# Attention tiles in whole 128-row products, with one pass of scores that is turned, in a fused two-layer mixer and expert kernel

## The chip, the core and the metric

The kernel runs on one core of a Trainium2 chip. A core has TensorE (matrix products, out of SBUF into PSUM), VectorE, ScalarE and GpSimd for elementwise work, and DMA queues, most of them issued by SyncE. The metric is device time in microseconds of one execution of the whole program.

## The reference, cut to what matters

The program computes a block with three mixers side by side (an RWKV-7 recurrence, a sparse attention with three branches called NSA here, and a memory attention), an output projection, a second mixer, and 64 routed experts. Sequence 1024, width 1024; the query is handled in tiles of 128 rows, 8 in all. The change lies in the two attentions. With four heads of width 64:

```python
# compressed branch: 63 compressed keys
s_c = einsum('bqhd,bcd->bhqc', qn, k_cmp) * scale
p_c = masked_softmax(s_c, cmp_end <= tq)
o_c = einsum('bhqc,bcd->bqhd', p_c, v_cmp)
# selected branch: top 16 of 16 blocks of 64 keys, so all earlier keys
p_s = masked_softmax(einsum('bqhd,bqkd->bhqk', qr, kg) * scale, kpos <= tq)
o_s = einsum('bhqk,bqkd->bqhd', p_s, vg)
# local branch: a window of 512 keys
p_w = masked_softmax(einsum('bqhd,bkd->bhqk', qr, kwb) * scale, m_w)
o_w = einsum('bhqk,bkd->bqhd', p_w, vwb)
o = g0 * o_c + g1 * o_s + g2 * o_w          # then a norm per head and a gate
# memory attention: 256 keys, four heads of their own
prob = softmax(einsum('bthd,bmhd->bhtm', q, mem_k) * scale)
o = einsum('bhtm,bmhd->bthd', prob, mem_v)
```

## The kernel before, in words

**Streams.** The sequence is worked in two halves of 512 rows (H = 0, 1). Each piece of work is a generator that yields an estimate of its cost; `weave` always advances the generator whose sum of costs, times its rate, is lowest. So the costs behind `yield` set the order in which instructions are written down; outside the blocks under `manual_schedule` the engines' queues alternate more finely than the yields. Three weaves concern attention: in the first, `first_stage(0)` runs alone (projections of the recurrence, `derive`); in the second, `att_proj(0)`, `mem_kv`, `first_stage(1)` and `att_proj(1)` run beside `recur(0)` and `attend(0)`; in the third, `third_stage(0)` (output projection and second mixer of the first half) runs beside `recur(1)` and `attend(1)`, until these two end. `attend(H)` runs `mem_tile(i)` and `nsa_tile(i)` for the four query tiles i of its half. Then follow the rest of both halves, the router, and the experts, whose weights (64 x 3 x 2 MB) are loaded by `load_piece` (L1676). The first three of these loads wait for the router's index table of the first half (`idx0`); the experts' rows are gathered once the routing of both halves is known.

**Number forms.** A matrix product on data marked F32R is one pass; on F32 it is recorded as two instructions. To keep accuracy, operands are split in a high part rounded to F32R and the rest: `qh`, `ql` for queries (L954, L956), `ph`, `pl` for probabilities (L1064 to L1067). Keys of the selected and local branch, `ksT` and `kwT`, hold the high part in rows 0 to 63 and the rest in rows 64 to 127, and the queries hold the head twice, so that one product of 128 rows sums both.

**mem_tile.** Queries `mq` come as two pairs of heads, a head in each half of the rows. Scores (L916) are F32 products of 64 rows and 256 columns, four a tile; then a maximum, an exponential with its sum (L921), eight transposes (L930) and the product with the memory values (L937).

**nsa_tile, compressed branch.** Scores `pc` (L965) are F32 products of 64 rows against `kcT`, four a tile in two groups; softmax on all heads; two transposes (L977); the product `poc` with `vcm` (L985) is again four products of 64 rows, copied by ScalarE (L986).

**nsa_tile, selected and local branch.** With nb key blocks of 128 (i + 1 selected, at most 5 local; over all tiles 36 and 30), keys are cut in one chunk, or in two when nb is over 4. First pass, per head and chunk (L1012 to L1020): scores `pmx`, query by key, from `qh` and `ql`, a mask product on the last block (and the first of a full window), the negated maximum on VectorE, and an exponential on ScalarE, back into PSUM, of which only the sum is kept. The maxima of the 16 rows (two branches, four heads, high and low parts) are then transposed (L1038) and spread in a table `nmb` (L1044). Second pass, per block (L1057 to L1067): scores `pS`, key by query for four heads (512 columns), from `qh`, `ql` and a product of `ones` with `nmb`, which subtracts the maxima, and on 20 blocks in all a mask (L1061); the exponential is taken twice, rounded (`ph`) and full (`pf`), and the difference is `pl`. Both are multiplied with `vsw` (L1050), which holds the values' high part in 64 columns and the rest in the other 64, and summed over the blocks in `po`. At the end of a branch the two halves of `po` are added (L1077, L1078), four 64-row transposes turn the result (L1082), and it is weighted and added to `o`.

**Buffers.** Scores and turned pieces use the PSUM tag "s" (two banks), sums the tag "o" (one). SBUF tag "acc" has three buffers, "ph" and "pl" two each.

## Time and profile before

| what | value |
|---|---|
| median of 3 runs | 2548.81 us (2540.53 to 2549.47) |
| profiled execution | 2546.94 us, its span 2544.8 us |
| TensorE busy over the span | 2423.5 us (95%), 13518 products |
| VectorE, ScalarE, GpSimd busy | 1550.0 (61%), 772.7 (30%), 348.5 us (14%) |
| mean granted clock of TensorE | 0.979 |
| DMA | 603.67 MB, mean 237 GB/s |

Times in the trace count from the start of the span. Attention runs from about 300 to 970 us; the seam between the second and the third weave lies at 630 to 655 us. A matmul's length includes the drain of the array, and matmuls overlap, so the sum of lengths is not the time that they take from each other; the distance between starts is.

### The profile page before, as it was taken

What the parts mean: (1) busy time and instruction counts of PE and PEld (TensorE: products, weight loads), DVE (VectorE), ACT (ScalarE), POOL (GpSimd) and SP (SyncE); (2) the same over time, 40 slices, a digit from 0 to 9 for tenths busy, and PEclk for the clock granted to TensorE, in tenths of its full rate; (3) what the DMA queues carried; (4) which work ended last, traced back from release to release, by engine and by line L of the source; (5) the groups of instructions that cost most, each with busy time, mean ns of one, the idle gap of its engine ahead of it and who ended that gap; (6) DMA issues with size and microseconds to landing.
All of it is one profiled execution on the core that took longest, in us unless ns stands there. A gap on an engine that the chain in (4) does not pass through costs nothing. (4 is left out here: it accounts for less than half of the span.)

```text
span 2544.8 us, 36038 instructions
## 1 busy us (share of the span) xinstructions
PE 2423.5 (95%) x13518; PEld 1545.9 (61%) x13518; DVE 1550.0 (61%) x3104; ACT 772.7 (30%) x1516; POOL 348.5 (14%) x464
## 2 busy tenths in 40 slices
PE   8989999999988999999999969999999999999997
PEld 6766777777756767887878834444444444444443
DVE  5537666665776776676665646555555555555555
ACT  4423544434436543334242321111111111111112
POOL 3000000000001011101120020111111111111112
PEclk9989999999888999999999979999999999999999
DMA  7666544443523222445345668999999999999992
GB/s 166 163 148 192 144 106 123 109 121 94 177 59 117 73 70 71 133 136 170 116 139 196 248 237 358 410 408 412 412 409 412 410 408 412 410 410 408 408 410 84
DMA packets 352078, 603.67 MB, mean 237 GB/s; under 512 B 124408, under 2 KB 298112, under 8 KB 327328
## 3 DMA queue, kind: packets, MB, share of 16 engines
q1 hardware_dynamic: 344496, 592.53, 64.9%
q0 software_dynamic: 5168, 8.69, 1.1%
q8 instruction: 108, 1.77, 0.3%
q14 instruction: 66, 0.54, 0.1%
q10 hardware_dynamic: 2240, 0.14, 0.1%
HBM read 562.54 MB, written 47.25 MB: 240 GB/s over the span
## 5 line engine op out<-in xcount | busy, mean ns | idle before, releaser
L1738 PE MATMUL pgu<-mw,xT 128*64 128x512 f32 x2048 | 460.9, 597 | 2.3 <-DVE up L1743 2.3
L277 PE MATMUL pcm<-hTh,whi 128*128 128x512 f32 (+1 forms) x912 | 370.1, 406 | 0.2 <-DVE hTl L265 0.2
L277 PE MATMUL pcm<-hTh,wlo 128*128 128x512 f32 (+1 forms) x912 | 362.9, 398 | 0.4 <-DVE wlo L238 0.4
L277 PE MATMUL pcm<-hTl,whi 128*128 128x512 f32 (+1 forms) x912 | 360.8, 396 | 0.0
L237 ACT ACTIVATE whi<-wraw 128x512 fp32r<-128x512 f32 (+1 forms) x300 | 187.2, 625 | 458.8 <-PE pcm L277 318.0
L238 DVE TENSOR_TENSOR wlo<-wraw,whi 128x512 fp32r<-128x512 f32 (+1 forms) x300 | 211.4, 708 | 181.0 <-ACT whi L237 159.2
L1738 PEld LDWEIGHTS pgu<-mw,xT 128*64 128x64 f32 x2048 | 142.7, 137 | 265.6 <-issue 254.7
L1796 DVE TENSOR_TENSOR mw<-psp,mw 128x1024 f32<-128x1024 f32 x248 | 292.5, 1220 | 8.8 <-PE psp L1788 5.1
L1788 PE MATMUL psp<-yo,wt 128*128 128x512 f32 x1024 | 274.9, 410 | 4.1 <-DVE mw L1796 3.2
L1788 PEld LDWEIGHTS psp<-yo,wt 128*128 128x128 f32 x1024 | 182.8, 188 | 139.0 <-issue 80.6
L1766 PE MATMUL pyd<-mw,hT 128*64 128x512 f32 x1008 | 229.9, 598 | 2.3 <-DVEq L1929 2.3
L1742 DVE SCALAR_TENSOR_TENSOR mth<-mth,pgu 64x512 f32<-64x512 f32 x64 | 43.4, 679 | 291.6 <-ACT mth L1741 291.6
L277 PEld LDWEIGHTS pcm<-hTh,whi 128*128 128x128 f32 (+1 forms) x912 | 170.6, 187 | 41.4 <-issue 6.2
L277 PEld LDWEIGHTS pcm<-hTl,whi 128*128 128x128 f32 (+1 forms) x912 | 170.8, 187 | 39.3 <-issue 6.2
L277 PEld LDWEIGHTS pcm<-hTh,wlo 128*128 128x128 f32 (+1 forms) x912 | 170.2, 187 | 40.1 <-issue 2.3
L1741 ACT ACTIVATE mth<-pgu,rq 64x512 f32<-64x512 f32 x64 | 43.8, 684 | 491.8 <-PE pgu L1738 491.8
L1773 ACT ACTIVATE yo<-pyd,gt 64x512 fp32r<-64x512 f32 x128 | 87.6, 684 | 305.6 <-PE pyd L1766 304.3
L1775 DVE SCALAR_TENSOR_TENSOR yo<-pyd,gt,yo 64x512 fp32r<-64x512 f32 x128 | 95.9, 749 | 126.5 <-ACT yo L1773 125.4
L1781 POOL TENSOR_SCALAR wt<-rcon,tfs 128x128 fp32r<-128x128 f32 x256 | 150.3, 608 | 149.1 <-PE psp L1788 125.4
L1766 PEld LDWEIGHTS pyd<-mw,hT 128*64 128x64 f32 x1008 | 66.9, 136 | 126.7 <-issue 123.2
L1800 POOL DMA_INDIRECT xg<-d_x,idxt x32 | 34.4, 1074 | 688.6 <-issue 630.4
L1170 PE MATMUL pout<-whi,yh 128*128 128x512 f32 x256 | 107.7, 421 | 3.0 <-DVE rr L1173 3.0
(492 smaller groups left out, 3464.3 us busy)
## 6 DMA issues: line engine op xcount, KB each, us to landing
mw<-in_w_gate_dram SPq DMA_DIRECT2D x64, 2048.0 KB, 13.7
mw<-in_w_up_dram SPq DMA_DIRECT2D x64, 2048.0 KB, 9.6
mw<-in_w_down_dram SPq DMA_DIRECT2D x63, 2048.0 KB, 14.4
wraw<-in_w_in_dram SPq DMA_DIRECT2D x216, 256.0 KB, 3.2
wraw<-in_w_out_dram SPq DMA_DIRECT2D x32, 256.0 KB, 2.8
yr<-d_y SPq DMA_DIRECT2D x32, 256.0 KB, 3.0
d_x<-rr SPq DMA_DIRECT2D x16, 512.0 KB, 2.8
wraw<-in_w_o_dram SPq DMA_DIRECT2D x32, 256.0 KB, 2.9
```

The costliest lines, as they stand in the source:

```text
L237: nc.scalar.activation(hi, raw, AF.Copy)
L238: nc.vector.tensor_sub(lo, raw, hi.bitcast(F32))
L277: nc.tensor.matmul(ps[0:n], w, h[:, k], start=(k == 0 and j == 0), stop=(k == KD - 1 and j == 2))
L1170: nc.tensor.matmul(ps, y[:, t], w, start=(k == 0 and j == 0), stop=(k == 1 and j == 2))
L1738: nc.tensor.matmul(ph_[lohi[s]], xT[:, k], pieces[s][:, k * 512:(k + 1) * 512], start=(k == 0), stop=(k == KD - 1))
L1741: nc.scalar.activation(th, ph_[0:64], AF.Tanh, scale=rq[:, 0, h:h + 1])
L1766: nc.tensor.matmul(py[s][lohi[s]], hT[:, k, lohi[h]], piece[:, k * 1024 + s * 512:k * 1024 + s * 512 + 512], start=(k == 0), stop=(k == 3))
L1773: nc.scalar.activation(y[:, 0, 512 * s:512 * s + 512], py[s][o], AF.Copy, scale=gt[o, h:h + 1])
L1775: nc.vector.scalar_tensor_tensor(y[:, 1, 512 * s:512 * s + 512], py[s][o], gt[o, h:h + 1], y[:, 0, 512 * s:512 * s + 512].bitcast(F32), op ...
L1781: nc.gpsimd.tensor_scalar(w[0:n, i], iota[0:n], sh[0:n, i:i + 1], None, op0=OP.is_equal)
L1788: nc.tensor.matmul(ps[:, cs], w[0:n], yo[0:n, x, cs], start=(start and x == 0), stop=(x == 1))
L1796: nc.vector.tensor_tensor(x2, ps, x2, op=OP.add)
```

## The change: what it does

- Memory branch: queries are stored per head, the head twice (as for the selected branch), and split in `qh`, `ql` by a new helper `queries`; memory keys hold the high part and the rest in 128 rows. Scores are F32R products of 128 rows.
- Compressed branch: `kcT` and `vcm` are filled as block diagonals of two heads, so that one product of 128 rows serves two heads.
- Selected and local branch: the second pass is gone. The exponentials of the first pass are kept in SBUF; for each pair of heads and pair of blocks they are transposed into PSUM (`pTs`), split in `ph` and `pl` there, and multiplied with `vsw` in products of 256 columns. Each chunk has its own sum `po`, which is copied whole, turned by four 128-row transposes, and its halves are added then. Two chunks are joined by weights at the end of the branch.
- Beside that: `pa` in `derive` uses 128 rows, the lower half of its weights cleared by GpSimd; the table of maxima, `ones` and the transposed masks go; the compressed keys share a buffer with `Pw`; a junk tile moves.

```diff
     def derive(H, p, lora, tw, rest):
...
+        nc.gpsimd.memset(up[0:64, 1], 0.0)
...
-        nc.tensor.matmul(pa_, up[64:128, 1], lora[64:128], start=True, stop=True)
+        nc.tensor.matmul(pa_, up[:, 1], lora, start=True, stop=True)
...
     def compress(H):
...
+        kcv = wk1.tile([P, 16 + H2], F32, tag="Pw", name="kcv")
...
-        nc.vector.tensor_copy(kcT[H][:, 0:n], pk[:, 0:n])
+        for r in range(2):
+            nc.vector.tensor_copy(kcT[H][lohi[r], 64 * r:64 * r + n], pk[lohi[r], 0:n])
...
     def att_proj(H):
...
-            nc.sync.dma_start(d_mq[ts, :, c].rearrange("n q t -> q n t"), by_tile(s))
+            for b in range(2):
+                for o in lohi:
+                    nc.sync.dma_start(d_mq[ts, o, 2 * c + b].rearrange("n q t -> q n t"), by_tile(s[lohi[b]]))
...
+    def queries(src):
+
+        qd = at.tile([P, 4 * P], F32, tag="acc", name="qd", bufs=4)
+        nc.sync.dma_start(qd, src.rearrange("q h t -> q (h t)"))
+        qh = at.tile([P, 4 * P], F32R, tag="qh", name="qh")
+        nc.scalar.activation(qh, qd, AF.Copy)
+        ql = at.tile([P, 4 * P], F32R, tag="ql", name="ql")
+        nc.vector.tensor_sub(ql, qd, qh.bitcast(F32))
+        return qh, ql
+
     def mem_tile(i):
...
-            for c in range(2):
-                nc.tensor.matmul(ps[:, c * 256:(c + 1) * 256], mq[lohi[e], c], memk[lohi[e], c], start=True, stop=True)
+            for x in range(2):
+                h = 2 * j + x
+                for q in (qh, ql):
+                    nc.tensor.matmul(ps[:, x * 256:(x + 1) * 256], q[:, h * P:(h + 1) * P], memk[:, h],
+                                     start=q is qh, stop=q is ql)
...
     def nsa_tile(i):
...
-        for e in range(2):
-            ps = S1("pc")
-            for c in range(2):
-                nc.tensor.matmul(ps[:, c * 64:(c + 1) * 64], qn[lohi[e], c], kcT[H][lohi[e]], start=True, stop=True)
...
+        ps = S1("pc")
+        for c in range(2):
+            nc.tensor.matmul(ps[:, c * P:(c + 1) * P], qn[:, c], kcT[H], start=True, stop=True)
...
+        poc = S1("poc")
+        for c in range(2):
+            nc.tensor.matmul(poc[:, c * P:(c + 1) * P], pcT[:, c], vcm[H], start=True, stop=True)
...
+            for n, (u, v) in enumerate(zip(cut, cut[1:])):
...
+                po = O1("poT")
+                ready = []
+
+                def with_v():
+                    j, bs, parts = ready.pop(0)
+                    for k, b in enumerate(bs):
+                        for p_ in parts:
+                            nc.tensor.matmul(po[:, 256 * j:256 * j + 256], vsw[:, s0 + u + b, br], p_[:, 256 * k:256 * k + 256],
+                                             start=(b == 0 and p_ is parts[0]), stop=(b == v - u - 1 and p_ is parts[1]))
+                    return 0.302 * len(bs)
+
+                for j in range(2):
+                    prs = []
+                    for h in (2 * j, 2 * j + 1):
...
+                        m = mx[:, br, n, h:h + 1]
+                        nc.vector.tensor_reduce(m, ps[:, 0:w], axis=AX.X, op=OP.max, negate=True)
+                        pr = at.tile([P, 4 * P], F32, tag="acc", name="pr", bufs=4)
+                        nc.scalar.activation(pr[:, 0:w], ps[:, 0:w], AF.Exp, bias=m, accum_out=sm[:, br, n, h:h + 1])
+                        prs.append(pr)
+                        yield 0.2 * (v - u) + 0.2
+                        if ready:
+                            yield with_v()
+                    for g in range(0, v - u, 2):
+                        bs = range(g, min(g + 2, v - u))
+                        pt = S1("pTs")
+                        for k, b in enumerate(bs):
+                            for x in range(2):
+                                nc.tensor.transpose(pt[:, (2 * k + x) * P:(2 * k + x + 1) * P], prs[x][:, b * P:(b + 1) * P],
+                                                    ident)
+                        c = 256 * len(bs)
+                        ph, pl = [at.tile([P, 4 * P], F32R, tag=t, name=t, bufs=2) for t in ("ph", "pl")]
+                        nc.scalar.activation(ph[:, 0:c], pt[:, 0:c], AF.Copy)
+                        nc.vector.tensor_sub(pl[:, 0:c], pt[:, 0:c], ph[:, 0:c].bitcast(F32))
+                        yield 0.3 * len(bs)
+                        if len(ready) > 0:
+                            yield with_v()
+                        ready.append((j, bs, (ph, pl)))
+                yield 0.5
+                while ready:
+                    yield with_v()
+                oS = at.tile([P, 4 * P], F32R, tag="pl", name="oS", bufs=2).bitcast(F32)
+                nc.scalar.activation(oS, po, AF.Copy)
+                yield 0.3
+                pt = S1("pob")
+                for h in range(4):
+                    nc.tensor.transpose(pt[:, h * P:(h + 1) * P], oS[:, h * P:(h + 1) * P], ident)
...
-        for br, kT in enumerate((ksT, kwT)):
-            s0 = b0 if br else 0
-            nc.vector.tensor_tensor(nmb[0:16], nms[:, None, :].to_broadcast([16, 4, P]),
-                                    nsel[:, br, :, None].to_broadcast([16, 4, P]), op=OP.mult)
-            po = O1("poT")
...
-                nc.tensor.matmul(ps, blk, qh, start=True, stop=False)
-                nc.tensor.matmul(ps, blk, ql, start=False, stop=False)
-                nc.tensor.matmul(ps, ones, nmb.rearrange("p h t -> p (h t)"), start=False, stop=mask is None)
...
-                nc.scalar.activation(ph, ps, AF.Exp)
...
-                nc.scalar.activation(pf, ps, AF.Exp)
-                nc.vector.tensor_sub(pl, pf, ph.bitcast(F32))
```

## Rows read from the trace of the kernel before

**Rows 1.** Stretches: window, length; busy PE, PEld, DVE, ACT, POOL; PEclk, DMA share, GB/s.

```profile
300.00:630.00 330.00, 326.10 (x2214) 245.58 (x2213) 208.25 (x473) 149.69 (x330) 25.41 (x20) 0.99 0.43 108
630.00:655.00 25.00, 16.22 (x89) 12.83 (x89) 10.59 (x24) 8.10 (x18) 2.01 (x2) 0.66 0.64 207
655.00:810.00 155.00, 139.55 (x895) 99.59 (x893) 118.22 (x299) 79.10 (x181) 8.07 (x10) 0.90 0.36 107
810.00:970.00 160.00, 156.87 (x1144) 111.30 (x1143) 116.80 (x264) 85.03 (x199) 17.70 (x14) 1.00 0.25 71
970.00:1490.00 520.00, 501.87 (x2787) 410.99 (x2786) 338.09 (x735) 175.41 (x336) 65.17 (x70) 0.99 0.48 155
1550.00:2545.00 995.00, 966.30 (x4332) 438.31 (x4330) 554.42 (x807) 153.66 (x232) 186.62 (x296) 1.00 0.94 386
```

**Rows 2.** Timeline, TensorE, 831 to 832.6 us: start, length, line, operation, shapes, count.

```profile
831.37 0.66 PE L965 MATMUL pc<-kcT,qn 64*128 64x64 f32 x4
831.95 0.50 PE L277 MATMUL pcm<-hTh,whi 128*128 128x512 f32 x1
832.29 0.39 PE L277 MATMUL pcm<-hTl,whi 128*128 128x512 f32 x1
832.52 0.40 PE L277 MATMUL pcm<-hTh,wlo 128*128 128x512 f32 x1
```

**Rows 3.** Timeline, TensorE, 662 to 664 us.

```profile
663.51 0.28 PE L1012 MATMUL pmx<-ksT,qh 128*128 128x256 f32 x1
663.63 0.28 PE L1013 MATMUL pmx<-ksT,ql 128*128 128x256 f32 x1
```

**Rows 4.** Timeline, TensorE, 442 to 448 us.

```profile
443.31 0.44 PE L900 MATMUL pfin<-cst,on 128*128 128x128 f32 x2
443.68 1.90 PE L916 MATMUL pM<-memk,mq 64*128 64x256 f32 x8
445.51 0.50 PE L277 MATMUL pcm<-hTh,wlo 128*128 128x512 f32 x1
445.85 0.40 PE L277 MATMUL pcm<-hTh,whi 128*128 128x512 f32 x1
...
446.78 0.60 PE L930 MATMUL pTm<-cst,prm 128*128 128x128 f32 x4
447.13 0.48 PE L277 MATMUL pcm<-hTl,whi 128*128 128x512 f32 x1
447.45 0.40 PE L277 MATMUL pcm<-hTh,wlo 128*128 128x512 f32 x1
```

**Rows 5.** Timeline, TensorE, 623 to 625 us.

```profile
623.92 0.39 PE L1061 MATMUL pS<-maskb,identb 128*128 128x512 bf16 x1
623.96 0.58 PE L1050 MATMUL poT<-ph,vsw 128*128 128x512 f32 x1
624.38 0.39 PE L1050 MATMUL poT<-pl,vsw 128*128 128x512 f32 x1
```

**Rows 6.** Groups, TensorE, 285 to 970 us: shapes, count, busy us, mean ns.

```profile
L1059 PE MATMUL pS<-nmb,ones 128*128 128x512 f32 x66 | 26.4, 414 | 0.0
...
L1061 PE MATMUL pS<-maskb,identb 128*128 128x512 bf16 x20 | 7.8, 390 | 0.0
```

**Rows 7.** Timeline, TensorE, 517.2 to 518.8 us.

```profile
517.60 0.46 PE L1082 MATMUL pob<-cst,oS 64*128 64x64 f32 x4
517.99 0.50 PE L1057 MATMUL pS<-qh,kwT 128*128 128x512 f32 x1
```

**Rows 8.** Groups, all engines, 285 to 970 us.

```profile
L1067 DVE TENSOR_TENSOR pl<-pf,ph 128x512 fp32r<-128x512 f32 x66 | 45.6, 690 | 38.8 <-ACT pf L1066 34.5 <-PE pS L1059 3.5 <-PE pS L1058 0.5
...
L1066 ACT ACTIVATE pf<-pS 128x512 f32<-128x512 f32 x66 | 39.5, 599 | 0.0
```

**Rows 9.** Stretches, columns as in rows 1.

```profile
462.70:466.20 3.50, 2.89 (x28) 1.93 (x26) 3.45 (x9) 0.60 (x1) 0.00 (x0) 1.00 0.49 121
466.20:469.60 3.40, 3.40 (x7) 2.06 (x7) 3.39 (x9) 1.00 (x2) 0.00 (x0) 0.50 0.79 204
```

More of the change, by code (lines that the diff above doesn't have):

```diff
@@ L164, in body @@
     maskb = const.tile([P, _GOFF[1] - _GOFF[0]], BF, name="maskb")
[L165 removed]
+    causb, edgeb, beforeb, onesb = [maskb[:, x * P:(x + 1) * P] for x in range(4)]
     mhalf = const.tile([P, 64], F32, name="mhalf")
@@ L485, in body @@
     gl = res.tile([P, NT, 12], F32, name="gl")
-    kcv = res.tile([P, 16 + H2], F32, name="kcv")
+    kcl = res.tile([P, 16], F32, name="kcl")
     cact = res.tile([P, 64], F32, name="cact")
-    kcT, vcm = [[res.tile([P, 64], F32, name=f"{n}{H}") for H in range(2)] for n in ("kcT", "vcm")]
+    kcT, vcm = [[res.tile([P, P], F32, name=f"{n}{H}") for H in range(2)] for n in ("kcT", "vcm")]
     hgain = vcol(4)
@@ L564, in att_proj @@
         if H == 0:
-            for x in range(0, 6, 3):
-                masks = put()[:, 0:3 * P]
-                nc.sync.dma_start(masks, a["cst"][:, _GOFF[0] + x * P:_GOFF[0] + (x + 3) * P])
-                nc.vector.tensor_copy(maskb[:, x * P:(x + 3) * P], masks)
+            masks = put()
+            nc.sync.dma_start(masks, a["cst"][:, _GOFF[0]:_GOFF[1]])
+            nc.vector.tensor_copy(maskb, masks)
         rope = wk1.tile([P, 2, H2], F32, tag="xr", name="rope", bufs=2)
@@ L1004, in nsa_tile @@
             cut = [0, nb] if nb <= 4 else [0, (nb + 1) // 2, nb]
-            for h in range(4):
-                q = slice(h * P, (h + 1) * P)
-                for n, (u, v) in enumerate(zip(cut, cut[1:])):
-                    ps = S1("pmx")
-                    w = (v - u) * P
-                    ends, starts = v == nb, br == 1 and i >= 4 and u == 0
-                    rhs = kT[:, (s0 + u) * P:(s0 + v) * P]
-                    nc.tensor.matmul(ps[:, 0:w], qh[:, q], rhs, start=True, stop=False)
-                    nc.tensor.matmul(ps[:, 0:w], ql[:, q], rhs, start=False, stop=not (ends or starts))
-                    if starts:
-                        nc.tensor.matmul(ps[:, 0:P], identb, edgeb, start=False, stop=not ends)
-                    if ends:
-                        nc.tensor.matmul(ps[:, w - P:w], identb, causb, start=False, stop=True)
-                    m = mx[:, br, h, n:n + 1]
-                    nc.vector.tensor_reduce(m, ps[:, 0:w], axis=AX.X, op=OP.max, negate=True)
-                    nc.scalar.activation(ps[:, 0:w], ps[:, 0:w], AF.Exp, bias=m, accum_out=sm[:, br, h, n:n + 1])
-                yield 0.25 * nb
@@ L1022, in nsa_tile @@
-            if len(cut) > 2:
+            outs = []
+            for n, (u, v) in enumerate(zip(cut, cut[1:])):
+                w = (v - u) * P
+                ends, starts = v == nb, br == 1 and i >= 4 and u == 0
+                rhs = kT[:, (s0 + u) * P:(s0 + v) * P]
+                po = O1("poT")
[7 more added lines that the diff above has]
+                    return 0.302 * len(bs)
+                for j in range(2):
+                    prs = []
+                    for h in (2 * j, 2 * j + 1):
+                        q = slice(h * P, (h + 1) * P)
+                        ps = S1("pS")
+                        nc.tensor.matmul(ps[:, 0:w], qh[:, q], rhs, start=True, stop=False)
+                        nc.tensor.matmul(ps[:, 0:w], ql[:, q], rhs, start=False, stop=not (ends or starts))
+                        if starts:
+                            nc.tensor.matmul(ps[:, 0:P], identb, edgeb, start=False, stop=not ends)
+                        if ends:
+                            nc.tensor.matmul(ps[:, w - P:w], identb, causb, start=False, stop=True)
+                        m = mx[:, br, n, h:h + 1]
[10 more added lines that the diff above has]
+                        for k, b in enumerate(bs):
+                            for x in range(2):
+                                nc.tensor.transpose(pt[:, (2 * k + x) * P:(2 * k + x + 1) * P], prs[x][:, b * P:(b + 1) * P],
[17 more added lines that the diff above has]
+                    nc.tensor.transpose(pt[:, h * P:(h + 1) * P], oS[:, h * P:(h + 1) * P], ident)
+                pt = pt.rearrange("p (h x d) -> p h x d", h=4, x=2)
+                t = at.tile([P, 4, 64], F32, tag=("sc", "sqh")[n], name="ob")
+                nc.scalar.activation(t, pt[:, :, 0], AF.Copy)
+                nc.vector.tensor_tensor(t, pt[:, :, 1], t, op=OP.add)
+                outs.append(t)
+                yield 0.2
@@ L1087, in nsa_tile @@
+                nc.vector.tensor_tensor(m, sm[:, br, 0], sm[:, br, 1], op=OP.add)
+                weight(br + 1, m)
+                for n, t in enumerate(outs):
+                    nc.vector.tensor_tensor(mb[:, n], mb[:, n], den[:, :, br + 1], op=OP.mult)
+                    nc.vector.tensor_tensor(t, t, mb[:, n, :, None].to_broadcast([P, 4, 64]), op=OP.mult)
+            for t in outs:
+                nc.vector.tensor_tensor(o, o, t, op=OP.add)
         yield from finish_heads(i, o, 0)
```

125 lines of the change are left out of this document (33 added, 92 removed).

## The prediction, made before the changed kernel was run

> **What bounds the kernel now.** Read the stretches first [rows 1]. The columns that matter are TensorE's busy time, its granted clock and the DMA share. From 300 to 630 us TensorE is busy 326 of 330 us at a clock of 0.99; the other engines reach at most two thirds (VectorE 208 us, ScalarE 150). So the first half of attention is a queue of matmuls: what leaves that queue leaves the time. The same holds from 810 to 970 (157 of 160) and, for the stage behind attention, from 970 to 1490 (502 of 520). Between 630 and 655 (clock 0.66) and between 655 and 810 (140 of 155 us, clock 0.90) TensorE is not full: there the seam between the streams and the waits of attention on VectorE and ScalarE count too. From 1550 on the DMA engines are busy 0.94: the expert weights set the pace. Their loads wait for the routing, so that part starts as much earlier as attention ends earlier, and all of a gain or loss in front arrives at the end. The last chain of waits lies behind all this and says nothing of attention.
>
> The profiled execution took 2546.9 us (span 2544.8); the median of the three runs is 1.9 us above it. I make the sum against 2546.9 and add 1.9 at the end.
>
> **Prices.** "Busy" of a matmul includes its drain, so I price by the distance from one start to the next. A product of 512 columns costs 0.23 us (832.29 to 832.52 in [rows 2]), one of 256 columns 0.12, even where the weights change from qh to ql [rows 3]. Four 128x128 transposes take 0.35 us, and the product behind them 0.32 instead of 0.23: 0.44 together, 0.11 each [rows 4]. No row shows a 64-row product cheaper than one of 128 rows and as many columns, and it costs at both ends of its group: two transposes that should take 0.22 take 0.37 in front of one, and the 512-column product behind one takes 0.34 [rows 2, 4]. I take 0.2 us for entering and leaving. A mask over 512 columns shares 0.46 us with the next product, so it costs 0.23 [rows 5].
>
> **The sum on TensorE**, before to after:
> 1. The second pass of scores (L1057 to L1061) goes. It ran on 66 key blocks, with the products qh, ql and the maxima, 3 x 512 columns, and on 20 of them a mask [rows 6]. 66 x 3 x 0.23 + 20 x 0.23 = 50.1 us less. The first pass (L1012 to L1017) stays; its exponentials, of the same widths, go to SBUF now and are used.
> 2. These lie query by key and must be turned: four transposes a block, 264 x 0.11 = 29.0 us more.
> 3. The products with V have the same columns in pieces of 256: 264 x 0.12 - 132 x 0.23 = 1.3 us more.
> 4. The output is turned in whole rows, and once for each chunk: 24 chunks (two a branch in tiles 4 to 7, one in tiles 0 to 3) x 4 x 0.11 = 10.6 us, for 16 groups at 0.39 [rows 7] + 0.2 = 9.4: 1.2 us more.
> 5. Compressed scores: two groups of four fp32 instructions, 0.58 [rows 2] + 0.2 each, become four of 128 columns. The fp32 instruction of 256 columns took 1.83 / 8 = 0.23 [rows 4], so 128 columns are 0.115: 0.46. 8 tiles x (1.56 - 0.46) = 8.8 us less. Their product with V is one group in the code, priced as one of the above: 8 x (0.78 - 0.46) = 2.6 less.
> 6. Memory scores: 1.83 + 0.2 us [rows 4] of fp32 in 64 rows become eight single-pass products of 256 columns, 0.96: 8 x 1.07 = 8.6 less.
> 7. The eight `pa` products get 128 rows: 8 x 0.2 = 1.6 less. The transposed maxima (8 transposes) are under 1 us and left out.
> Sum: -50.1 + 29.0 + 1.3 + 1.2 - 8.8 - 2.6 - 8.6 - 1.6 = **-40.2 us** of TensorE.
>
> **The other engines.** ScalarE drops two exponentials of 512 columns a block, 132 x 0.60 = 79 us [rows 8], and gets a copy for each turned pair of blocks: counted from the chunk sizes there are 54 groups of 512 columns and 24 of 256, at most 78 x 0.60 = 47. Output copies (24 of full height for 16 of half, and 24 of 256 columns) and memory queries (8) add some 20, so it does not end above its load of before. VectorE drops 66 subtractions of 0.69 [rows 8] and gets at most 78; it loses the table of maxima and gets 8 query subtractions and some 24 additions of 256 columns. It ends within some 20 us of its 454 from 300 to 970 [rows 1], far from TensorE's load in the full stretches. These I cost at nothing: TensorE's queue covers them. Without that cover a chunk would show one exponential, one copy, one subtraction and one output copy in a row, 0.60 + 0.60 + 0.69 + 0.60 = 2.5 us [rows 8]; the two copies have no row and are bounded by the exponential of their width.
>
> DMA and queues: the memory queries are written twice over in four 128 KB stores for one (16 issues in all on SP's queue instead of 4) and read as 256 KB; SP runs loads ahead, and the DMA share is 0.43 and less in attention [rows 1], so this is hidden. The copy and subtraction of the memory queries put 1.3 us ahead of a tile; other products cover it in seven tiles, and in the seam at 630 to 655 it shows once. GpSimd's eight clears of 64 rows lie on an engine that is busy 25 of 330 us [rows 1]. The compressed keys now share a buffer with the decay factors of the recurrence's inputs; between their uses lie whole projections, nothing waits. Smaller mask and junk tiles cost nothing.
>
> **What does not arrive.** In 655 to 810 TensorE waits, so work removed there may only lengthen a wait. Tiles 4 and 5, which lie there, hold 21 of the 66 blocks and two of the eight sets of fixed savings: 21 x (0.69 - 0.44) + 2 x 2.5 + 6 masks x 0.23, about 12 us. I give up between nothing and all of it, and take 5 with the 1.3 of the seam: -35 us. 2546.9 - 35 = 2512, and **2514 us** on the scale of the median. Giving up all of it would be -28, nothing -40.
>
> **Rivals.**
> A. The chain of a chunk shows. One pass has more steps in a row than a second pass that needs only maxima: exponential, turn, copy, product, output copy, turn. For it: 655 to 810 already has waits, and there are two score banks. Price: all 16 chunks of tiles 4 to 7 at 2.5 us = 40, which eats the gain: 2548.8 - 40 + 40 = 2549. Against it: between 810 and 970 projections stand ready and TensorE stayed at 157 of 160 with a similar chain.
> B. The clock, on the good side. In 462.7 to 466.2 the engine ran 28 products, 24 of them of 64 rows (L965, L750), busy 2.9 of 3.5 us, and in the next stretch the clock was 0.50, the lower of its levels, 1.2 of 2.4 GHz [rows 9]. If whole products hold it up, the 0.10 missing in 655 to 810 (15.5 us) comes back besides the full 40: 2548.8 - 40 - 15.5 = 2493.
> C. The clock, on the bad side. 264 transposes and fewer products make the queue thinner. If the clock of the seam, 0.66 [rows 1], held through the 160 us of tiles 6 and 7, that stretch would grow by 160 x (1 / 0.66 - 1) = 82 us: 2548.8 - 40 + 82 = 2591. It turns the sign for a measurement from about 106 us at half clock, which is what 40 + 13 us cost. Against it: behind the four transposes at 446.78 the products keep to full-speed distances [rows 4], and the turns lie between such products. The Trainium skill (TensorE: Matmul & The Clock Gate, Part 4: PE-mode transpose) says that transposes do not count as activity for the clock as other products do; by that rule C gains, and the time would be the 2591 of this case. The trace neither bears this out nor contradicts it: no row shows transposes for long without other products.
> That the change leaves the second pass in is excluded by the diff.
>
> **Chances and range.** 2514 has 0.60, B 0.20, A 0.12, C 0.08. The range goes from B's end to A's side of the forecast's own unknowns (a quarter of the gain left): 2492 to 2540. A measurement of this kernel tells 0.5%, 12.7 us, from no change. The forecast and B lie beyond it (faster 0.80), A within (0.12), C slower (0.08).
>
> **What would show it.** In the changed profile TensorE's instructions of the score pass should be as many as in the first pass before, with 264 transposes at about 0.11 us from start to start, and no 512-column products of the maxima. Attention should end near 935 us instead of 970, and the stage behind it should keep its length. TensorE should stay over 0.95 busy in 300 to 630. Waits of the turns on ScalarE's exponentials, of several tenths a chunk, would mean A; a granted clock under 0.90 behind 655 would mean C; a clock of 1.00 there, B. An end of attention that stays at 970 with a lower TensorE busy time would make the prediction wrong; so would an equal shift that the weight stream gives back.

## The result and the profile after

The kernel after takes 2520.23 us (median of 4 runs, 2515.48 to 2521.22) against 2548.73 us for the kernel before beside it (2540.53 to 2549.47). The ratio is 0.9894, with a 95% interval of 0.9877 to 0.9911: 28.5 us less, where 35 were forecast. The profiled execution has a span of 2519.4 us, 25.4 less than before. TensorE's busy time fell from 2423.5 to 2386.9 us with 13656 products for 13518; VectorE has 1543.9 us, ScalarE 754.7, and the mean granted clock is 0.978. The ratios below leave out two executions of one experiment, e2, which took 2887 and 3030 us at mean clocks of 0.79 and 0.74.

To see where the time came from I cut both executions at the same events: the first product of the memory attention, the first product of the output projection, and the last product of the recurrence (which ends the third weave). First the kernel before, by stretches (columns as in [rows 1]):

```profile
0.00:303.40 303.40, 274.60 (x1889) 212.88 (x1889) 174.03 (x383) 119.73 (x223) 36.51 (x43) 0.96 0.66 166
303.40:650.00 346.60, 333.92 (x2254) 252.44 (x2254) 214.11 (x487) 152.92 (x337) 27.42 (x22) 0.98 0.45 117
650.00:1033.50 383.50, 363.67 (x2634) 263.55 (x2634) 277.34 (x661) 179.94 (x409) 35.56 (x32) 0.95 0.30 86
1033.50:2544.80 1511.30, 1451.33 (x6752) 817.02 (x6746) 884.51 (x1576) 320.11 (x549) 249.04 (x367) 0.99 0.81 318
```

Then the kernel after, cut at the same events:

```profile
0.00:300.60 300.60, 270.89 (x1889) 210.77 (x1890) 176.13 (x385) 120.19 (x225) 37.30 (x49) 0.97 0.66 169
300.60:633.20 332.60, 315.96 (x2274) 250.82 (x2273) 205.88 (x473) 146.57 (x324) 27.38 (x24) 0.98 0.47 124
633.20:1006.80 373.60, 347.49 (x2749) 265.14 (x2749) 277.75 (x679) 167.99 (x391) 36.14 (x32) 0.95 0.31 89
1006.80:2519.40 1512.60, 1452.52 (x6756) 818.67 (x6750) 884.12 (x1576) 319.99 (x549) 248.75 (x367) 0.99 0.81 317
```

The four lengths change by -2.8, -14.0, -9.9 and +1.3 us. In the two middle ones TensorE lost 18.0 and 16.2 us of busy time, of which 4.0 and 6.3 turned into idle time. The last stretch keeps its length but for 1.3 us, so what is gained in front arrives at the end.

The fixed stretches that answer to [rows 1], and the worst 40 us, of the kernel after; last, the same 40 us of the kernel before:

```profile
300.00:630.00 330.00, 315.52 (x2271) 250.24 (x2270) 204.96 (x471) 146.26 (x325) 26.37 (x23) 0.98 0.46 122
655.00:810.00 155.00, 134.45 (x997) 101.91 (x998) 119.53 (x307) 75.68 (x177) 12.72 (x14) 0.88 0.35 101
810.00:970.00 160.00, 156.57 (x1306) 119.35 (x1305) 113.71 (x274) 72.23 (x173) 18.21 (x15) 1.00 0.26 73
700.00:740.00 40.00, 29.95 (x133) 23.12 (x133) 36.17 (x101) 13.43 (x34) 3.59 (x3) 0.83 0.19 53
700.00:740.00 40.00, 35.53 (x217) 23.01 (x215) 32.92 (x91) 12.76 (x28) 2.65 (x2) 0.95 0.27 79
```

TensorE is still a full queue from 300 to 630 (0.956 busy) and from 810 to 970. Between 655 and 810 it has 134.5 us for 140 in the same 155, at a clock of 0.88 for 0.90. Between 700 and 740 it is VectorE that is full: 36.2 of 40 us (32.9 in the kernel before).

The groups of the new form (line, engine, operation, tiles, shapes, count, busy us, mean ns, idle before):

```profile
L1048 PE MATMUL pTs<-cst,pr 128*128 128x128 f32 x264 | 47.6, 286 | 5.6 <-ACT pr L1038 5.5
L1020 PE MATMUL poT<-ph,vsw 128*128 128x256 f32 x132 | 41.8, 325 | 3.2 <-ACT ph L1052 2.5
L1020 PE MATMUL poT<-pl,vsw 128*128 128x256 f32 x132 | 38.2, 309 | 2.2 <-DVE pl L1053 2.1
L1053 DVE TENSOR_TENSOR pl<-pTs,ph 128x512 fp32r<-128x512 f32 x54 | 36.3, 688 | 26.0 <-ACT ph L1052 25.5
```

There are 264 turns and 132 + 132 products with V in pieces of 256 columns, as counted; the second pass of [rows 6] is gone. And TensorE's longest waits from 633 to 1007 us (line, waited for, us in total, times, longest):

```profile
PE pTs L1048 <- ACT pr L1038: 5.5, 8, 2.3
PE pout L1171 <- DVE rr L1174: 5.1, 2, 3.3
PE pfin L898 <- DVE on L894: 4.0, 4, 1.5
PE pfin L898 <- DVE om L894: 3.3, 3, 2.2
```

The turns wait for exponentials, the output projection for VectorE to add up its rows, and the last turn of a tile (`pfin`) for VectorE's norm. These are short, but some have a second price, which the experiments show. Waits of this kind are not all new. The kernel before has two at places that are gone (300 to 1010 us): its score pass on the exponentials in the score banks, and the turn of the maxima.

```profile
PE pmx L1012 <- ACT pmx L1020: 3.4, 7, 1.0
PE pmr L1038 <- DVE nrs L190: 3.3, 1, 3.3
```

### The profile page after: what moved, and what is told of

Read it like the earlier page. It is cut to its first block, busy times and chain, and to the rows that moved or that the text cites. A ratio compares the mean times of both kernels' runs of the same rounds, so it can differ in the third digit from the quotient of the medians.

```text
span 2519.4 us, 36225 instructions
## 1 busy us (share of the span) xinstructions
PE 2386.9 (95%) x13656; PEld 1545.4 (61%) x13656; DVE 1543.9 (61%) x3112; ACT 754.7 (30%) x1488; POOL 349.6 (14%) x472
## 5 line engine op out<-in xcount | busy, mean ns | idle before, releaser
L272 PEld LDWEIGHTS pcm<-hTh,whi 128*128 128x128 f32 (+1 forms) x912 | 170.8, 187 | 39.1 <-issue 5.4
L1743 ACT ACTIVATE mth<-pgu,rq 64x512 f32<-64x512 f32 x64 | 43.8, 684 | 493.4 <-PE pgu L1740 493.4
L1802 POOL DMA_INDIRECT xg<-d_x,idxt x32 | 34.4, 1076 | 690.0 <-issue 630.9
```

Source lines behind the costliest of these rows:

```text
L272: nc.tensor.matmul(ps[0:n], w, h[:, k], start=(k == 0 and j == 0), stop=(k == KD - 1 and j == 2))
L1743: nc.scalar.activation(th, ph_[0:64], AF.Tanh, scale=rq[:, 0, h:h + 1])
```

## The experiments

**How the runs are read.** From the first memory product to the last product of the recurrence, a length is split in three: idle time of TensorE; what the clock cost, taken as half of the busy time inside the spells at granted clock 0.50; and the rest, "work", the busy time as it would be at full clock. Half is taken because a 512-column product then needs twice its time. Four starts around the end of such a spell, timeline of the kernel after:

```profile
633.90 0.63 PE L1171 MATMUL pout<-wlo,yh 128*128 128x512 f32 x1
634.33 0.63 PE L1171 MATMUL pout<-whi,yh 128*128 128x512 f32 x1
...
635.28 0.39 PE L1171 MATMUL pout<-whi,yh 128*128 128x512 f32 x1
635.51 0.39 PE L1171 MATMUL pout<-wlo,yh 128*128 128x512 f32 x1
```

0.43 us from start to start in the spell, 0.23 behind it. The table holds all runs (the split comes from one profiled execution each, the ratio from the timed runs against the kernel before):

| kernel | ratio, 95% interval | length | work | clock | idle |
|---|---|---|---|---|---|
| before | | 730.1 | 675.6 | 22.0 | 32.5 |
| after | 0.9894 (0.9877 to 0.9911) | 706.2 | 643.5 | 19.9 | 42.8 |
| e1 one pass alone | 1.0067 (1.0045 to 1.0088) | 747.2 | 657.8 | 49.2 | 40.2 |
| e2 compressed alone | 0.9929 (0.9906 to 0.9953) | 708.3 | 666.1 | 9.8 | 32.4 |
| e3 memory alone | 1.0001 (0.9989 to 1.0013) | 727.6 | 671.1 | 19.8 | 36.7 |
| e4 `pa` alone | one execution | 725.1 | 675.4 | 16.9 | 32.8 |
| e8 one pass, compressed | 1.0029 (1.0019 to 1.0039) | 735.1 | 653.4 | 42.2 | 39.5 |
| e11 one pass, memory | 0.9995 (0.9986 to 1.0004) | 720.8 | 654.9 | 25.3 | 40.6 |
| e5 turned twice | 1.0027 (1.0017 to 1.0037) | 735.1 | 674.4 | 21.6 | 39.1 |
| e6 no subtraction | 0.9844 (0.9828 to 0.9860) | 687.7 | 638.8 | 12.1 | 36.7 |
| e7 no low half | 0.9791 (0.9775 to 0.9807) | 679.5 | 621.5 | 18.5 | 39.5 |
| e9 substitution on GpSimd | 0.9917 (0.9904 to 0.9930) | 709.0 | 646.0 | 15.6 | 47.4 |
| e10 later norm | 0.9924 (0.9909 to 0.9939) | 710.8 | 643.5 | 26.7 | 40.6 |
| e12 attention slower | 0.9935 (0.9922 to 0.9948) | 712.7 | 640.8 | 28.1 | 43.8 |

How far a single split can be trusted shows in the runs themselves. With TensorE's products unchanged, work came out 4.7 us lower in e6, 2.7 lower in e12 and 2.5 higher in e9. And the kernel before, in 17 executions beside e1, took 2537.6 to 2552.9 us at mean clocks of 0.983 to 0.976. So differences under some 5 us in the columns for work and clock mean little by themselves.

**The theory and its rivals.** Mine: TensorE's time is the sum of the parts, and the 12 us or so that did not arrive were lost where the chain of a chunk is longer, in the one-pass part. Rivals: every part loses the same share; or the 64-row forms and the clock pay differently from what I priced.

### e1 to e4: one part at a time

e1, the kernel before with the one-pass part:

```diff
-                    ps = S1("pmx")
+                        ps = S1("pS")
...
-                    nc.scalar.activation(ps[:, 0:w], ps[:, 0:w], AF.Exp, bias=m, accum_out=sm[:, br, h, n:n + 1])
+                        nc.scalar.activation(pr[:, 0:w], ps[:, 0:w], AF.Exp, bias=m, accum_out=sm[:, br, n, h:h + 1])
...
+                                nc.tensor.transpose(pt[:, (2 * k + x) * P:(2 * k + x + 1) * P], prs[x][:, b * P:(b + 1) * P],
+                                                    ident)
```

> The kernel before with the one-pass selected and local branches alone; compressed and memory branches and pa stay in 64-row form (two junk tiles of the row norms share another buffer, for room, at no cost). My sum for this part: 50.1 - 29.0 - 1.3 - 1.2 = 18.6 us less of TensorE. Theory 1, the missing part of the gain is lost here alone, because one pass has the longer chain: the time falls by 6 to 10 us. Theory 2, every part loses the same share (28.5 of 40.2 us arrived, 0.71): it falls by 13 us. Theory 3, 64-row forms cost more than my prices and the turns too: it falls by under 5 us, and TensorE's busy time by under 12.

It is slower, by 17 us (0.67%), which no theory had. The work fell by 17.8 us, as counted; but the clock cost 27.2 us more than before and idle time 7.7. Stretches of e1, each line with a pause or a spell:

```profile
721.80:725.20 3.40, 0.72 (x4) 0.26 (x2) 3.40 (x13) 0.04 (x1) 0.00 (x0) 1.00 0.00 0
725.60:739.30 13.70, 13.47 (x37) 9.40 (x37) 9.27 (x23) 2.64 (x9) 0.73 (x1) 0.50 0.17 50
746.10:763.20 17.10, 14.44 (x43) 10.28 (x43) 10.89 (x35) 3.84 (x10) 0.00 (x0) 0.50 0.09 24
766.60:793.90 27.30, 22.41 (x145) 16.16 (x147) 15.45 (x36) 20.33 (x39) 4.66 (x7) 0.50 0.50 166
927.00:930.40 3.40, 1.31 (x7) 0.72 (x6) 2.86 (x5) 0.00 (x0) 3.32 (x3) 1.00 0.39 136
930.40:950.90 20.50, 20.50 (x156) 16.16 (x155) 8.91 (x22) 5.26 (x14) 1.15 (x2) 0.50 0.28 80
```

In the first line VectorE is full and TensorE is busy for 0.72 us of 3.40; then the clock falls to its lower level, 1.2 of 2.4 GHz. At 927 us a single wait stands ahead of it, behind a row of projections (timeline of e1):

```profile
927.07 0.39 PE L277 MATMUL pcm<-hTh,whi 128*128 128x512 f32 x1
929.55 0.41 PE L896 MATMUL pfin<-cst,on 128*128 128x128 f32 x2 [2.09 <-DVE on L892]
```

Behind this wait of 2.09 us the engine runs 20.5 us without a gap (20.50 busy) at half clock, some 10 us lost. The profiled execution, 2567.3 us, lies 5.6 us above the median of e1's runs. The mean clock of e1's six timed runs is 0.965 to 0.970, of the kernel before beside it 0.976 to 0.983, so this belongs to the kernel and not to one execution.

e2, the kernel before with the compressed part:

```diff
-        for e in range(2):
-            ps = S1("pc")
-            for c in range(2):
-                nc.tensor.matmul(ps[:, c * 64:(c + 1) * 64], qn[lohi[e], c], kcT[H][lohi[e]], start=True, stop=True)
+        ps = S1("pc")
+        for c in range(2):
+            nc.tensor.matmul(ps[:, c * P:(c + 1) * P], qn[:, c], kcT[H], start=True, stop=True)
```

> The kernel before with the compressed branch alone in 128-row products. My sum: 8.8 + 2.6 = 11.4 us less of TensorE. Theory 1 (the loss lies in the one-pass part): the time falls by 10 to 12 us. Theory 2 (every part loses the same share): by 8 us. Theory 3 (64-row forms cost more than priced, through the clock or the drain): by over 14 us.

It is 18 us faster (12 to 24), more than all of its 11.4 us. The work fell by 9.5, and the clock gave back 12.2: where the kernel before has four spells between 655 and 810 us, e2 has one. In the profiled execution the clock took 5.2 us of this back ahead of the first memory product and 3.3 behind the recurrence.

By the distance between starts (halved in the spells), the scores `pc` fell from 8.9 to 3.7 us, and the product `poc` only from 4.8 to 3.5. A row of the kernel before shows why there was little to win at `poc`:

```profile
838.54 0.67 PE L985 MATMUL poc<-vcm,pcT 64*128 64x64 f32 x8
839.13 0.50 PE L277 MATMUL pcm<-hTh,wlo 128*128 128x512 f32 x1
```

Eight instructions of `poc` take 0.59 us, as long as the four of `pc` in [rows 2] (0.58). In the trace they start in pairs 0.01 us apart, while those of `pc`, one half of the rows at a time, start 0.11 apart; where both groups of `pc` come together (656.2 us), they pair as well. So it looks as if products in the two halves run side by side; which half each instruction belongs to the trace does not say.

e3, the kernel before with the memory part:

```diff
-    memk = res.tile([P, 2, 256], F32, name="memk")
+    memk = res.tile([P, 4, 256], F32R, name="memk")
...
+                for q in (qh, ql):
+                    nc.tensor.matmul(ps[:, x * 256:(x + 1) * 256], q[:, h * P:(h + 1) * P], memk[:, h],
+                                     start=q is qh, stop=q is ql)
```

> The kernel before with the memory branch alone in 128-row products of high and low halves (and the shared buffer of the compressed keys, for room). My sum: 8.6 us less of TensorE; against it stands the copy and subtraction ahead of a tile, 1.3 us, that I took as covered. Theory 1: the time falls by 8 to 9 us. Theory 2: by 6 us. Theory 3: by over 11 us.

No change. The work fell by 4.5 us, half of what I had summed, and 4.2 of it became idle time. By the distance between starts the memory scores fell from 15.2 to 9.0 us and the turns in front of them by 1.3, 7.5 us together; the rest lies at other products, within the error of the split.

e4, the kernel before with the `pa` products in 128 rows:

```diff
+        nc.gpsimd.memset(up[0:64, 1], 0.0)
...
-        nc.tensor.matmul(pa_, up[64:128, 1], lora[64:128], start=True, stop=True)
+        nc.tensor.matmul(pa_, up[:, 1], lora, start=True, stop=True)
```

> The kernel before with the eight pa products alone in 128 rows. My sum: 1.6 us. Theories 1 and 2: the recurrence's inputs end 1 to 2 us earlier, and TensorE's busy time before attention falls by as much. Theory 3 (64-row groups cost more than the 0.2 us I gave them): by 3 us or more. The time of one execution cannot tell these apart; the place of the first product of the recurrence's inputs of each chunk in the trace can.

The timeline of the kernel before around one of them, and under it that of e4:

```profile
46.72 0.40 PE L277 MATMUL pcm<-hTh,whi 128*128 128x512 f32 x1
47.04 1.12 PE L428 MATMUL pa<-lora,lup 64*128 64x512 f32 x2
48.09 0.50 PE L277 MATMUL pcm<-hTl,whi 128*128 128x512 f32 x1
48.43 0.40 PE L277 MATMUL pcm<-hTh,wlo 128*128 128x512 f32 x1
```

```profile
45.98 0.40 PE L277 MATMUL pcm<-hTh,whi 128*128 128x512 f32 x1
46.21 1.06 PE L429 MATMUL pa<-lora,lup 128*128 128x512 f32 x2
46.70 0.79 PE L277 MATMUL pcm<-hTl,whi 128*128 128x512 f32 x1
47.33 0.39 PE L277 MATMUL pcm<-hTh,wlo 128*128 128x512 f32 x1
```

From the product before to the second one behind are 1.71 us in 64 rows (46.72 to 48.43) and 1.35 in 128 (45.98 to 47.33). So a whole-row product saves 0.36 us, not 0.2, and the eight 2.9, not 1.6. At the other three groups of the first half the distances are the same to 0.01 us. The first product of the rotated halves (L580, in e4 L581) comes at 152.5 us for 155.2; four `pa` groups ahead of it explain 1.4 of these 2.7 us.

**What the four say together.** Work adds up: -17.8, -9.5, -4.5 and -0.2 make -32.0 us, and the kernel after has -32.1. Idle time nearly does: 7.7, -0.1, 4.2 and 0.3 make +12.1, against +10.3. The clock does not: 27.2, -12.2, -2.2 and -5.1 make +7.7, against -2.1. The times add least of all: +17, -18 and 0 us, and -3 in e4's one execution, make -4, where the whole change has -28.5. Part of that lies behind the recurrence: with the same products there, the last stretch of e1, e2 and e3 is 1514.7 to 1516.7 us long with 8.8 to 10.6 us lost to the clock, and that of the kernel before 1511.3 with 5.7.

### e8 and e11: pairs, to see which part holds the clock

e8 joins the edits of e1 and e2, e11 those of e1 and e3.

> The kernel before with the one-pass part and the compressed part together (the two parts of e1 and e2; the memory branch and pa keep their 64-row products). TensorE's work at full clock fell by 17.8 us in e1 and by 9.5 in e2 between the first memory product and the last product of the recurrence; if work adds up, it falls by 27 us here. On the clock the theories part. Own-loss theory (one pass with its turns costs clock by itself): the 27 us that e1 lost at half clock stay, and the time is within 10 us of the kernel before. Half-height theory (the compressed branch's 64-row products are what pulls the clock down beside the turned chunks): the busy time at half clock falls to e2's 20 to 40 us, and the time is 25 to 35 us under the kernel before. Order theory (where TensorE's pauses fall is an accident of the instruction order): anything between, and each half-clock spell begins behind a pause of TensorE of over 1.5 us.

> The kernel before with the one-pass part and the memory part together (the compressed branch and pa keep their 64-row products). Work adds up so far: 17.8 and 4.5 us less of TensorE, 22 in all, between the first memory product and the last product of the recurrence. One pass alone lost 27 us to half clock, and 20 of these stayed when the compressed branch came with it. Theory M (the memory branch's 64-row products keep the clock down beside one pass): the busy time at half clock falls from e1's 98 us to the kernel after's 40, and the time is 15 to 25 us under the kernel before. Theory O (an accident of the order, so that the loss ends only when all parts are there): the loss stays above 15 us, and the time is within 8 us of the kernel before.

With the compressed part the loss mostly stays: clock 42.2 us, the time 7 us above the kernel before, as the own-loss theory had it. With the memory part most of it goes: the clock costs 25.3 us, 24 less than in e1. The timed runs say about half: the median of the mean clock is 0.968 in e1, 0.970 in e8, 0.974 in e11, and 0.979 in the kernel before. The time, though, is that of the kernel before and not 15 to 25 us less; the work fell by 20.7, but 8.1 became idle time, 3.3 stays with the clock, and the stretches ahead and behind add 7.0 (305.3 us for 303.4 and 1516.4 for 1511.3). So beside one pass it is mostly the memory branch that brings the clock back. What about it does so is open: it removes 64-row products, and it also moves everything behind it. One place can be followed. The last turn at 929.6 us in e1 waits 2.09 us, the same turn in e8 (917.4) 2.27, and a spell of 20.5 us follows each. In e11 (910.6) it waits 0.60 us and none follows, though the next 20 us hold much the same mix: 12.3 of 20.5 us in products of 128 rows, for 11.8 of 20.4 in e1.

The order theory's claim on pauses held nearly everywhere. In the fourteen traces 64 spells at half clock begin between 600 and 1015 us; 63 of them begin in or directly behind a pause of TensorE of 0.8 us to 13 us, or a few shorter ones. They last from 3.4 to 34.1 us, and how long is not told by the length of the pause. Nor does each pause bring a spell: of 45 pauses of 1 to 2 us that began at full clock 16 were directly followed by one, of 47 longer ones 42. Even the same wait differs: the last turn at 886.4 us in e4 waits 1.12 us and a spell of 10.2 us follows; in the kernel before, e2 and e3 it waits 1.12 us as well (at 895.9, 879.7 and 891.0), and none does.

The Trainium skill (TensorE: Matmul & The Clock Gate, A second HAM failure mode: psum-queue depth-cycling) tells of a kernel whose short idle times between groups of products made the clock swing between its levels. These traces agree with that part: 0.50 behind pauses, most of them of 1 to 4 us.

### e5: the turns twice

```diff
-                                nc.tensor.transpose(pt[:, (2 * k + x) * P:(2 * k + x + 1) * P], prs[x][:, b * P:(b + 1) * P],
-                                                    ident)
+                                for _ in range(2):
+                                    nc.tensor.transpose(pt[:, (2 * k + x) * P:(2 * k + x + 1) * P], prs[x][:, b * P:(b + 1) * P],
+                                                        ident)
```

> The kernel after with each of the 264 transposes of the probabilities issued twice into the same place. At 0.11 us each that is 29.0 us more of TensorE. Count theory (TensorE's queue sets attention, save in the stretch where it waits): the time grows by 22 to 29 us. Wait theory (the chain of a chunk on ScalarE and VectorE sets it, TensorE has room): by under 15 us. Clock theory (transposes do not hold up the clock): by well over 29 us, with a granted clock lower than 0.95 between 300 and 1010 us.

The time grows by 34 us against the kernel after (1.0027 for 0.9894), a little over the count theory's end. The work grows by 30.9 us over 264 turns, 0.117 each: my 0.11 holds. The clock costs 21.6 us for 19.9, and the granted clock of the stretch is 0.97 for 0.96 (the kernel after, then e5):

```profile
300.60:1006.80 706.20, 663.45 (x5021) 515.97 (x5021) 483.63 (x1152) 314.55 (x715) 63.52 (x56) 0.96 0.38 106
301.60:1036.70 735.10, 696.05 (x5290) 546.54 (x5288) 487.39 (x1152) 316.29 (x714) 62.89 (x56) 0.97 0.37 102
```

So 528 turns in place of 264 did not pull the clock down. The Trainium skill's rule that transposes do not count as activity (TensorE: Matmul & The Clock Gate, Part 4: PE-mode transpose) shows in no run here; between other products, which these turns always have beside them, it changes nothing.

### e6 and e7: VectorE's part in it

e6 leaves out the subtraction and multiplies the high half twice, e7 leaves out the low half altogether:

```diff
-                        nc.vector.tensor_sub(pl[:, 0:c], pt[:, 0:c], ph[:, 0:c].bitcast(F32))
...
-                        ready.append((j, bs, (ph, pl)))
+                        ready.append((j, bs, (ph, ph)))
```

(in e7 the last line has `(ph,)`).

> The kernel after without the 78 subtractions that make the low half of the turned probabilities; the high half is multiplied with V twice, so the low half's share is missing from the output and TensorE has the same products. VectorE loses 78 x 0.68 = 53 us. If VectorE lies on attention's path (the wait behind the missing 11 us), the time falls by 5 to 11 us. If TensorE and ScalarE set it: within 2 us of the kernel after.

> The kernel after without the low half of the probabilities: neither its subtraction nor its product with V, so the low half's share is missing from the output. TensorE loses 132 x 0.12 = 15.8 us, VectorE 53 us. Count theory: the time falls by 11 to 16 us against the kernel after. Wait theory (the chain of a chunk sets the pace): by under 6 us, with TensorE's idle time up by the rest.

e6 is 13 us faster than the kernel after with the same products on TensorE, a little over the 5 to 11 expected. So VectorE is on the path, though its load is far below TensorE's on average. Whether by its load or by this step of a chunk's chain is not separated; TensorE's waits on the subtraction itself add up to 1.8 us in the kernel after from 633 to 1007 us. Stretches of e6, 700 to 740 us and the third stretch of the cut:

```profile
700.00:740.00 40.00, 33.41 (x202) 25.20 (x201) 35.16 (x97) 19.40 (x43) 2.19 (x2) 1.00 0.24 77
630.30:988.30 358.00, 336.71 (x2751) 258.00 (x2751) 254.19 (x625) 166.55 (x391) 36.73 (x32) 0.97 0.33 93
```

Between 700 and 740 VectorE is as full as before, but it gets further: TensorE has 202 products there for 133, and no spell (clock 1.00 for 0.83). Of the 18.5 us in this execution 6.1 are idle time and 7.8 clock; the other 4.7 stand under work, within the split's error. e7 takes 13.6 us more (0.9791 for 0.9844) for the 132 products of 0.12 us, 15.8, which it lacks: what leaves TensorE's queue leaves the time, nearly whole. Against the kernel after it is 26 us faster, beyond the 11 to 16 of the count theory, which gave the subtractions no price.

### e9, e10 and e12: three tries at the pauses

e9 moves the triangular substitution that keeps VectorE full near 700 us to GpSimd; e10 writes the tile's last turn later; e12 spreads attention to the end of the recurrence:

```diff
+            eng = nc.gpsimd if H else nc.vector
-            nc.vector.tensor_tensor(sv, NTt[:, s, s + 1:32, None].to_broadcast([P, nt, nj]),
+            eng.tensor_tensor(sv, NTt[:, s, s + 1:32, None].to_broadcast([P, nt, nj]),
...
-        yield 1.5
+        yield 1.5 if i < TH else 5
...
-    weave((g0, 0, 1), (recur(1), 9.9, 1.618), (attend(1), 0.1, 0.554), until=(1, 2))
+    weave((g0, 0, 1), (recur(1), 9.9, 1.618), (attend(1), 0.1, 0.62), until=(1, 2))
```

> The kernel after with the 62 instructions of the second half's triangular substitution (the lines that write scr and Ti) on GpSimd instead of VectorE. They take 20.7 us of VectorE, which is busy 36.2 of 40 us between 700 and 740 us; GpSimd is busy under 5 us there, and takes about twice as long for one instruction. VectorE theory (the missing part of the gain waits on VectorE in 655 to 810 us): the time falls by 5 to 12 us against the kernel after, and the pauses of the output projection on the sum of its rows shrink. TensorE theory (chains of ScalarE and TensorE, or the clock alone, take the gain): within 3 us. Slower by over 5 us would say that the substitution itself is on the path to the recurrence.

> The kernel after with the cost written ahead of a tile's last turn raised from 1.5 to 5 in the second half, so that more of the other streams is put in front of that turn, which waits 1 to 2 us for VectorE in tiles 4 to 7. Pause theory (half-clock spells come from such pauses): the pauses of the last turn behind 655 us go, at least one half-clock spell with them, and the time falls by 3 to 8 us. Against it: the pauses move to the next instruction that is late, and the time stays within 3 us.

> The kernel after with the rate of the second half's attention raised from 0.554 to 0.62, so that its tiles spread to the end of the recurrence (attention ends at 966 us, the recurrence at 1007, and VectorE is nearly full between 655 and 740). VectorE theory (attention, output projection and substitution crowd VectorE there, and pauses and half clock follow): TensorE is idle less behind 633 us, and the time falls by 3 to 10 us against the kernel after. If the pauses only move: within 3 us. Slower by over 3 us if more pauses fall where no projection stands ready.

All three miss: 6, 8 and 10 us slower than the kernel after (0.9917, 0.9924, 0.9935 for 0.9894; the intervals of e9 and e10 overlap that of the kernel after). In e9 VectorE does come free, but the tile's norm takes its inverse root on GpSimd, and that now stands in GpSimd's queue among the substitution's steps. A stretch of e9, its GpSimd at 714 us, and TensorE's wait:

```profile
700.00:740.00 40.00, 20.54 (x86) 16.46 (x84) 13.32 (x25) 8.26 (x17) 25.40 (x43) 0.70 0.20 61
```

```profile
714.70 0.62 POOL L715 TENSOR_TENSOR Ti<-Ti,scr 128x231 f32<-128x231 f32 x1
715.28 1.02 POOL L189 TENSOR_TENSOR st<-st,mhalf 128x4 f32<-128x4 f32 x1
716.28 0.55 POOL L713 TENSOR_TENSOR scr<-NTt,Ti 128x220 f32<-128x220 f32 x1
```

```profile
717.16 0.69 PE L899 MATMUL pfin<-cst,on 128*128 128x128 f32 x2 [12.99 <-DVE on L895]
```

TensorE waits 12.99 us for it, so e9 replaced one full engine by another queue. It does not test VectorE's load, nor do its 6 us say that the substitution itself is on the path; a version with the root elsewhere was not tried. In e10 the last turn still waits (2.82 us at 721.6, 1.84 at 900.4), and the clock costs 26.7 us. In e12 VectorE is as full as before and the clock costs 28.1. None of the three beats the kernel after.

## Why the prediction was right, and where not

- **The bound.** Right: TensorE's queue set the stretches that are full, and the last stretch kept its length (1511.3 and 1512.6 us). The time was 2514 forecast, 2520 measured.
- **One pass for two (steps 1 to 4 of the sum).** Right: -18.6 forecast, -17.8 measured alone (e1). The price of a turn, 0.11, was 0.117 in e5.
- **The 64-row forms (steps 5 to 7).** The sizes were off. Compressed scores and product: -11.4 forecast, -9.5 of work (e2). Memory scores: -8.6 forecast, -4.5 of work, -7.5 by the distance between starts (e3). `pa`: -1.6 forecast, -2.9 by its spacing (e4). One price of 0.2 us for entering and leaving does not fit all of them, since `pa` saves 0.36 a group. And that no row shows a 64-row product cheaper than one of 128 rows does not hold for `poc`, whose instructions start in pairs: eight of 64 rows take 0.59 us, where eight of `pc` take two groups of 0.58. The code has two groups of `poc`, not one; that the price of one was near is luck. Over the first three stretches the work fell by 34.4 us (the first one gives 2.3), where the sum had 40.2.
- **VectorE at nothing.** The reason failed, that TensorE's queue covers VectorE. I set its load in whole stretches against TensorE's, and 655 to 810 us hides 40 us in which it is full, with the substitution, the output projection's sums and attention's reductions in one queue. e6 puts 13 us on its subtractions. That the change itself lost time there is not shown: VectorE's load in the third stretch is what it was (277.8 us for 277.3), and the kernel before without its own 66 subtractions was not run.
- **What does not arrive.** Mis-sized: 5 us given up (the seam's 1.3 among them), 11.2 us of new idle time. Waits of turns on exponentials (5.5 us, several tenths for each of the 16 chunks) are rival A's sign; they are a seventh of A's 40, and about what the two waits that are gone had cost (6.7). The clock gave 3.6 us over the first three stretches. Together -34.4 + 11.2 - 3.6 + 1.3 = -25.5 us, the 25.4 of the spans.
- **The clock, rivals B and C.** I let it stand or fall as one thing for the whole change, and for the whole change it stood: 19.9 us for 22.0. Part by part it did not. From the first memory product on it gave 12 us to the compressed part and took 27 from one pass, so a gain of B's kind shows in e2 and a loss of C's kind decides e1. B's cause, the whole products, is not shown, since the order of everything moves with them. C's cause, the turns, was wrong: e5 doubles them and the clock stays.
- **The marks.** Wrong in one: attention does not end near 935 but where it did, its last product with V starting at 966.2 us for 966.9. The prediction had named that end, with a lower TensorE busy time, as the sign that it is wrong. The order of the weave is written by costs, so attention keeps its place and the other streams get further meanwhile: the output projection starts at 633.2 for 650.0 and the recurrence ends at 1006.8 for 1033.5. The shift, not the end of one stream, was the mark to give. C's mark, a clock under 0.90 behind 655, is met by the letter (0.88 between 655 and 810, for 0.90 before) without C's loss. The rest held: 264 turns, no second pass, TensorE at 0.956 from 300 to 630.

In the profiled executions 25.4 us came of 35: the sum was 6 us too high, the idle time 6 us larger than what I gave up, the last stretch 1.3 us longer, and the clock gave 4 us. That the clock stayed near where it was is in part luck: the reason given against C held (the turns lie between other products), but alone and in pairs the parts cost up to 27 us or gave 12, and nothing in the prediction foresaw that. What stays open is why the memory branch brings the clock back beside one pass, and what makes the new idle time.

## What to carry to other kernels

Sum the products that leave TensorE's queue: that sum adds up over the parts of a change to within a few microseconds. Then look at each place where TensorE waits 1 us or more for another engine: in these traces such pauses were often, not always, followed by 3 to 34 us at half clock, half of which is lost, even where TensorE then ran without a gap. And measure a change whole as well as in parts: one of its parts lost 17 us alone and the change gained 28.

## What the runs showed that I had not expected

- One part of a good change was slower than the kernel before, with 17.8 us less work, through the granted clock (49.2 us lost to it for 22.0) and 7.7 us more of idle time.
- A wait of 2.09 us was followed by 20.5 us at a granted clock of 0.50 in which TensorE was busy without a gap; a wait of 1.41 us for the same turn in the kernel after (892.0) was followed by none.
- A product of 64 rows and 512 columns in two recorded instructions, between products of 128 rows, cost 0.36 us more than the same in 128 rows. But with both halves of the rows at work, as in `poc`, 64-row products started in pairs 0.01 us apart.
- The substitution's widest steps took 0.62 to 0.73 us on GpSimd and 0.42 on VectorE, but a dependent chain on a queue that others need cost TensorE 12.99 us at one place.
